# Delta-rule mixer: the finish of a head is cut in two, and its second half is issued behind the next head's q stage

## The chip, the core and the metric

The kernel runs on one core of a Trainium2 chip, as one program that computes one inference step of a small hybrid decoder. Its time is the device time of one execution in microseconds (us). Five engines work side by side, each through its own list of instructions in a fixed order: TensorE (PE in the rows) multiplies and transposes, VectorE (DVE) and ScalarE (ACT) do elementwise work, GpSimd (POOL) does a few elementwise instructions and issues DMA transfers, and SyncE (SP) only issues transfers. Where one engine needs another's result it waits on a semaphore, and everything behind the waiting instruction on that engine waits with it.

## The reference

Two layers, each a mixer and a feed-forward block. The change lies in the mixer of the first layer, the gated delta rule over 8 heads of 128, for a prompt of 1024 tokens and 8 sample sequences of 8 tokens (1088 columns in all):

```python
proj = h @ w_in                                   # q, k, v and a gate, 1024 columns each
qkv = silu(causal_dwconv(qkv, buf, conv_w, conv_b))
q = l2norm(q) * DK ** -0.5;  k = l2norm(k)
# per chunk: decay[i,j] = exp(G_i - G_j) for i >= j
A = strict_lower((k*beta) @ k.T * decay)
sol = triangular_solve(A + I, [v*beta, k*beta*exp(G)])     # uv, w
attn = (q @ k.T) * decay
def step(S, ...):                                 # over the chunks
    u = uv - w @ S
    o = (q*exp(G)) @ S + attn @ u
    S = S * exp(G_last) + kd.T @ u
o = rmsnorm(o, norm_g) * silu(gate)
out = o @ w_out
```

The last two lines are what the change concerns: the output of a head is normalized, gated, and goes to memory until all heads are there, and then the output projection reads it.

## The kernel before

Tokens lie along the columns, 1024 of the prompt and 64 of the samples. Weights and activations of the large products are split into a high and a low part, so each product is three matmuls (L113 to L115 in `dense`); those of the mixer's projections write the tile `pp` and are called plain matmuls here.

Each head is a generator, `gdn_head(h)`, with a `yield` between its stages, and `stage(h, n)` advances head h by n stages. The stages: S1 projects k. S2 loads the decay `dec` (L812), masks it on GpSimd (L814, `affine_select`), takes its exponentials on ScalarE (eight L818, one L819), forms Z from k and k, and transposes k. S3 is the q stage: it projects q, solves 16x16 triangles row by row on VectorE (L881, L883, closed by L884), sends the solution to memory and back in another layout (`td`, issued at L886, and `mg`, issued at L887, which waits for `td`), scales it on ScalarE (L897, L898), multiplies k by q (`pqk`, L905, L908) and applies the decay (L906, L909), transposes q (`pq`, L792) for its sums of squares (L803 on ScalarE) and multiplies q by its decay (L917). S4 projects v and the gate: v goes through a short convolution (L751 and L755 on ScalarE, L758 three times on VectorE), a silu as tanh (L764 on ScalarE) and product (L765 on VectorE), and nine transposes (`pv`, L792). S5 builds the block inverse from Z and `mg`. S6 is the scan over 8 chunks. S7 is the samples' part, with the state update in `sample_state` (`pus`, L716, added at L719), the spill of the samples' state (L1068), and `finish`.

`finish` has a reciprocal square root on VectorE in small steps (L85 to L91), scales the output by it (`ot`, L671, L672), transposes it (`pot`, L676, `pots`, L680), multiplies by the gate (L678, L682), splits the product into a high part (`oh`, L684 on ScalarE) and a low one (L685 on VectorE), and sends both to memory (L686, L687, issued by GpSimd). Small cuts of the modulation work (`adap`, L176, L184) are put in by `ada_step`.

The order of the loop: per head h, S3 and S4 of h, S1 of h+1, S5 of h, S2 of h+1, S6 and S7 of h. This is program order only. A scheduler takes the instructions as they become ready, with program order as the priority, and so writes one fixed list per engine: work of the projections of h+1 fills TensorE between the steps of h. Tiles come from pools with few buffers: PSUM has three of the tag `mx`, which `pus`, `pqk`, `pq`, `pot`, `pots` and `pv` share, and three of `mm` for the plain matmuls. `ot` and `oh` share one buffer, `D5`. The second layer's mixer uses the same `finish`.

Of the kernel before, what the change touches and what calls it, by code (L numbers as in the profile page):

```python
# [42 lines left out]
def trunk_kernel(ctx: ExitStack, tc: tile.TileContext, a: dict, o: dict):  # L43
    nc = tc.nc
# [6 lines left out]
    def big(tag, shape=(128, NTOK), dt=F32, name=None, bufs=None):  # L51
        return main.tile(list(shape), dt, tag=tag, name=name or tag, bufs=bufs or {"xp": 2, "wraw": 3, "whl": 3}.get(tag, 1))

    def small(tag, shape, dt=F32, bufs=1, name=None):
        return sm.tile(list(shape), dt, tag=tag, name=name or tag, bufs=bufs)

    def ps(tag, name=None):
        return psp.tile([128, 512], F32, tag=tag, name=name or tag, bufs={"mm": 3, "mx": 3, "rc": 2}[tag])
# [4 lines left out]
    def cload(name, shape, dt=F32):  # L63
        t = const.tile(list(shape), dt, name="c_" + name)
        nc.scalar.dma_start(out=t, in_=a[name])
        return t

    ident = cload("ident", [128, 128])
# [11 lines left out]
    def rsqrt(y, x, n, tag, p=128):  # L80

        t = small("nwt" + tag, [128, n], bufs=2)[:p]
        xh = small("nwx" + tag, [128, n], bufs=2)[:p]
        sh = small("nws" + tag, [128, n], I32, bufs=2)[:p]
        nc.vector.tensor_scalar(sh, x.bitcast(I32), 1, None, op0=ALU.logical_shift_right)  # L85
        nc.vector.tensor_scalar(y.bitcast(I32), sh, -1.0, float(0x5F3759DF), op0=ALU.mult, op1=ALU.add)
        nc.vector.tensor_scalar(xh, x, -0.5, None, op0=ALU.mult)
        for _ in range(3):
            nc.vector.tensor_tensor(t, y, y, op=ALU.mult)
            nc.vector.tensor_tensor(t, t, xh, op=ALU.mult)  # L90
            nc.vector.scalar_tensor_tensor(y, t, 1.5, y, op0=ALU.add, op1=ALU.mult)  # L91
# [113 lines left out]
    def mod(l, i):  # L205
        return mods[l][:, 8 * i:8 * i + 8, :]

    def fold_scale(l, i, kind, ms=slice(0, 8)):

        m = mod(l, i)[:, ms]  # L210
        nc.vector.scalar_tensor_tensor(
            m, m, 1.0, normw[:, kind, l, ms].unsqueeze(2).to_broadcast([128, ms.stop - ms.start, 9]), op0=ALU.add, op1=ALU.mult)
# [226 lines left out]
    for j in range(4):  # L439
# [6 lines left out]
        for g in GORD:  # L446
            t0, n = GRP[g][0], GP[g]
            sc, sh = mod(0, 1), mod(0, 0)
            pt = big("D10", [128, 2, 512], name="pnt")
            for m in range(2 * j, 2 * j + 2):  # L450
                t = pt[:, m % 2, :n]
                h = hgs[g][:, 0, m, :n]
# [208 lines left out]
    def finish(l, h, ot, ot_s, ss, qe, ncol, gt, ohl, otag):  # L661

        var = small("fvar", [128, 9])
        if qe is None:
            nc.vector.tensor_scalar(var, ss, 1.0 / 128, EPS, op0=ALU.mult, op1=ALU.add)
        else:
            nc.vector.scalar_tensor_tensor(var, ss, 1.0 / 128, qe, op0=ALU.mult, op1=ALU.add)
        rs = small("frs", [128, 9])
        rsqrt(rs, var, 9, "f")
        o3 = ot[:, :NT].rearrange("p (t d) -> p t d", d=128)  # L670
        nc.vector.tensor_tensor(o3, o3, rs[:, 0:8].unsqueeze(2).to_broadcast([128, 8, 128]), op=ALU.mult)  # L671
        nc.vector.tensor_scalar(ot_s, ot_s, rs[:64, 8:9], None, op0=ALU.mult)  # L672
        for b in range(2):
            pt = ps("mx", name="pot")
            for j in range(4):
                nc.tensor.transpose(pt[:, 128 * j:128 * j + 128], o3[:, 4 * b + j, :], ident)  # L676
            gg = gt[:, 512 * b:512 * b + 512]
            nc.vector.scalar_tensor_tensor(gg, pt, ncol, gg, op0=ALU.mult, op1=ALU.mult)  # L678
        pt = ps("mx", name="pots")
        nc.tensor.transpose(pt[:, :NS], ot_s, ident[:64, :64])  # L680
        gg = gt[:, NT:]
        nc.vector.scalar_tensor_tensor(gg, pt[:, :NS], ncol, gg, op0=ALU.mult, op1=ALU.mult)  # L682
        oh = big(otag, dt=F32R, name="oh")
        nc.scalar.activation(oh, gt, AF.Copy)  # L684
        nc.vector.tensor_tensor(gt, gt, oh.bitcast(F32), op=ALU.subtract)  # L685
        nc.gpsimd.dma_start(out=ohl[h][:, 0, :], in_=oh.bitcast(F32))  # L686
        nc.gpsimd.dma_start(out=ohl[h][:, 1, :], in_=gt)  # L687

    smask = cload("smask", [64, 8])
    smask4 = cload("smask4", [64, 4])  # L690
# [35 lines left out]
    gnorm = cload("gnorm", [128, 1])  # L726
# [41 lines left out]
    rest = [(0, i, k) for i in (2, 3, 4) for k in range(8)]  # L768
# [7 lines left out]
    def gdn_head(h):  # L776
# [62 lines left out]
        def evac_k(b, p):  # L839
# [3 lines left out]
            else:  # L843
# [22 lines left out]
            out=Zp, in_=zd[par].rearrange("t x -> (t x)").rearrange("(b y) -> b y", y=2064)[:, :2048].rearrange(  # L866
                "b (j i) -> b j i", i=128)[:, :, 0:16])
# [11 lines left out]
        for i in range(1, 16):  # L879
# [8 lines left out]
                            in_=td[par].rearrange("(t k) (r x) -> (k r) t x", k=8, x=32))  # L888
# [22 lines left out]
        qe = small("gqe", [128, 9], bufs=2)  # L911
# [24 lines left out]
        gt = A(3, "g")  # L936
# [129 lines left out]
        nc.vector.tensor_copy(ot_s, pos[:64, :128])  # L1066
        sample_state(S0, kd_s, u_s, eGLs[:, :, h], v)
        nc.gpsimd.dma_start(out=o["s_gdn"][:, h].rearrange("s k v -> k s v"), in_=S0)  # L1068
        finish(0, h, ot, ot_s, so, qe, gnorm[:, 0:1], gt, ohl0, "D5")

    heads = [gdn_head(h) for h in range(H)]

    def stage(h, n=1):
        for _ in range(n):
            if h < H:
                next(heads[h], None)
# [75 lines left out]
    for b in range(3):  # L1152
        pr = ps("mx", name="pgr")
        ts = [4 * b + j for j in range(4)] if b < 2 else [8]
        for j, t in enumerate(ts):
# [15 lines left out]
                        in_=zero[64:, :].unsqueeze(1).to_broadcast([64, 2, 64]))  # L1171
    X128 = big("D6", [128, 8, 128], name="X128")
    nc.gpsimd.memset(X128, 0.0)
    ohl0 = [drp.tile([128, 2, NTOK], F32, name=f"ohl0{h}") for h in range(H)]

    for h in range(H):
        stage(h, 2 if h else 3)
        stage(h + 1)
        stage(h)
        stage(h + 1)  # L1180
        stage(h, 2)
    fold_scale(0, 2, 1)
    fold_scale(0, 4, 2)
    hgs = out_proj(0, ohl0, 0, 2, 3, 4, "h1")
# [18 lines left out]
    hnorm = cload("hnorm", [128, 1])  # L1203
# [10 lines left out]
    ohl1 = [drp.tile([128, 2, NTOK], F32, name=f"ohl1{h}") for h in range(H)]  # L1214

    def hgrn_head(h):
        par = h % 2
        A = lambda i, name: big(f"A{2 * i + par}", name=name)
        if h:
            q, k, v, gt = A(0, "q"), A(1, "k"), A(2, "v"), A(3, "g")  # L1220
        else:
            q, k, gt = big("cv0", name="q"), big("cv1", name="k"), big("D9", name="g")
# [142 lines left out]
        for b in range(2):  # L1365
# [4 lines left out]
            for j in range(4):  # L1370
# [3 lines left out]
                else:  # L1374
                    nc.vector.scalar_tensor_tensor(Sa[:, t, :], Sa[:, t - 1, :], tot[:, t:t + 1], pu[:, 128 * j:128 * j + 128],
                                                   op0=ALU.mult, op1=ALU.add)
        nc.gpsimd.dma_start(out=o["p_hgrn"][h], in_=Sa[:, 7, :])
        ot = big("D4", [128, NT], name="ot")
        ot_s = small("ot_s", [64, 128])
        so = small("gso", [128, 9])  # L1380
# [22 lines left out]
        nc.vector.tensor_copy(ot_s, pos[:64, :128])  # L1403
        sample_state(S0, kt_s, vt_s, t8, v)
        nc.gpsimd.dma_start(out=o["s_hgrn"][:, h].rearrange("s k v -> k s v"), in_=S0)
        finish(1, h, ot, ot_s, so, None, hnorm[:, 0:1], gt, ohl1, "D4")

    for h in range(H):
        hgrn_head(h)
# [132 lines left out]
```

## Time and profile before

| | us |
|---|---|
| median of three runs | 3267.77 (3267.25 to 3277.91) |
| profiled execution | 3262.61 |
| its span | 3260.8 |
| TensorE busy in the span | 3151.2 (97%) |
| VectorE busy | 1659.1 (51%) |
| ScalarE busy | 1102.4 (34%) |
| GpSimd busy | 276.4 (8%) |

The rows of the section further below come from the profiled execution. Times in them count from the start of its span, and the delta-rule mixer lies at about 90 to 790 us. An idle stretch is written behind an instruction in brackets, with what ended it. The chain of work that ended last is 88% TensorE. One name is misleading: where GpSimd's L887 is said to be released by TensorE, the `td` transfer is what it needs by the code.

### The profile page before, as it was taken

To read this page: it belongs to the slowest core of one execution; us is meant where nothing else is said; L and a number is where in the kernel's file an instruction comes from. 1 tells how busy PE (TensorE), PEld (TensorE's weight loads), DVE (VectorE), ACT (ScalarE), POOL (GpSimd) and SP (SyncE) were. 2 spreads that over 40 slices of the span, in tenths; PEclk is the share of its full clock that TensorE was granted. 3 is DMA by queue.
4 is the path that set the end of the run, shared out by engine and by line. 5 is a ranking of instruction groups with operands and counts; after the bars stand their busy time and mean duration, and the time that the engine had idled before them with its cause. 6 is when DMAs were issued, how large, how long until landed. Compare 5 with 4: busy or idle time off the path is not lost.

```text
span 3260.8 us, 61807 instructions
## 1 busy us (share of the span) xinstructions
PE 3151.2 (97%) x25457; PEld 2933.6 (90%) x25457; DVE 1659.1 (51%) x3783; ACT 1102.4 (34%) x2640; POOL 276.4 (8%) x623
## 2 busy tenths in 40 slices
PE   7999999999899999999998999999999999999998
PEld 5888888888799999999996999999878999999997
DVE  6776777774742333333347555554475233334345
ACT  5444444443433312122234333333333332222222
POOL 0111111110100000000000000000010000000002
PEclk9999999999999999999998999999999999999999
DMA  6333333234322222222223111122521111111113
GB/s 206 99 106 100 102 103 98 79 118 158 97 76 83 84 82 88 82 88 81 92 61 106 64 61 58 59 78 74 199 91 50 46 47 43 46 46 46 41 61 108
DMA packets 164642, 277.94 MB, mean 85 GB/s; under 512 B 20064, under 2 KB 91488, under 8 KB 164360
## 3 DMA queue, kind: packets, MB, share of 16 engines
q1 hardware_dynamic: 145976, 236.28, 22.4%
q0 software_dynamic: 14976, 37.08, 3.8%
q8 instruction: 200, 3.28, 0.4%
q10 hardware_dynamic: 3408, 0.63, 0.1%
q14 instruction: 82, 0.67, 0.1%
HBM read 222.44 MB, written 51.43 MB: 84 GB/s over the span
## 4 chain that ended last, share of the span: by engine, by line
PE 88%; DVE 5%; ACT 2%; DMA 2%; issue 2%; POOL 1%; ACTq 0%; SPq 0%; DVEq 0%; POOLq 0%
PE pp L114 7%; PE pp L113 7%; PE pp L115 7%; PE pu L113 5%; PE pg L113 5%; PE pg L114 5%; PE pg L115 5%; PE pu L115 5%; PE pu L114 5%; PE pd L113 5%; PE pd L115 5%; PE pd L114 5%; PE pf L113 1%; PE pf L114 1%; PE pf L115 1%
## 5 line engine op out<-in xcount | busy, mean ns | idle before, releaser
L114 PE MATMUL pp<-h,wi 128*128 128x384 f32 (+1 forms) x1536 | 515.4, 336 | 1.0 <-DVE h L321 0.9
L113 PE MATMUL pp<-h,wi 128*128 128x384 f32 (+1 forms) x1536 | 515.0, 337 | 0.8 <-DVE q L1236 0.6
L115 PE MATMUL pp<-h,wi 128*128 128x384 f32 (+1 forms) x1536 | 513.1, 335 | 0.8 <-issue 0.8
L113 PE MATMUL pg<-h,wg 128*128 128x384 f32 (+1 forms) x1056 | 346.6, 329 | 0.0
L114 PE MATMUL pg<-h,wg 128*128 128x384 f32 (+1 forms) x1056 | 345.6, 328 | 0.8 <-DVE h L321 0.8
L113 PE MATMUL pu<-h,wu 128*128 128x384 f32 (+1 forms) x1056 | 346.3, 328 | 0.0
L115 PE MATMUL pg<-h,wg 128*128 128x384 f32 (+1 forms) x1056 | 346.0, 328 | 0.0
L115 PE MATMUL pu<-h,wu 128*128 128x384 f32 (+1 forms) x1056 | 344.8, 327 | 0.0
L114 PE MATMUL pu<-h,wu 128*128 128x384 f32 (+1 forms) x1056 | 344.3, 326 | 0.0
L113 PEld LDWEIGHTS pp<-h,wi 128*128 128x128 f32 x1536 | 290.1, 189 | 16.1 <-issue 10.0
L113 PE MATMUL pd<-mh,wd 128*128 128x384 f32 (+1 forms) x912 | 299.5, 330 | 0.0
L115 PE MATMUL pd<-mh,wd 128*128 128x384 f32 (+1 forms) x912 | 297.4, 326 | 0.0
L114 PE MATMUL pd<-ml,wd 128*128 128x384 f32 (+1 forms) x912 | 297.1, 326 | 0.0
L114 PEld LDWEIGHTS pp<-h,wi 128*128 128x128 f32 x1536 | 290.6, 189 | 6.2 <-DVE h L321 1.4
L115 PEld LDWEIGHTS pp<-h,wi 128*128 128x128 f32 x1536 | 290.3, 189 | 4.9 <-issue 2.9
L113 PEld LDWEIGHTS pu<-h,wu 128*128 128x128 f32 x1056 | 198.2, 188 | 7.8 <-issue 6.2
L113 PEld LDWEIGHTS pg<-h,wg 128*128 128x128 f32 x1056 | 199.0, 189 | 6.2 <-issue 4.9
L114 PEld LDWEIGHTS pg<-h,wg 128*128 128x128 f32 x1056 | 199.0, 189 | 2.5 <-issue 1.2
L624 DVE TENSOR_TENSOR facc<-facc,pd 128x384 f32<-128x384 f32 (+1 forms) x192 | 97.6, 510 | 203.1 <-PE pd L115 203.1
L115 PEld LDWEIGHTS pg<-h,wg 128*128 128x128 f32 x1056 | 199.1, 189 | 0.0
L115 PEld LDWEIGHTS pu<-h,wu 128*128 128x128 f32 x1056 | 198.2, 188 | 0.0
L114 PEld LDWEIGHTS pu<-h,wu 128*128 128x128 f32 x1056 | 198.2, 188 | 0.0
(463 smaller groups left out, 5693.9 us busy)
## 6 DMA issues: line engine op xcount, KB each, us to landing
adaw<-in_ada_w SPq DMA_DIRECT2D x96, 512.0 KB, 3.8
wgr<-in_w_gu SPq DMA_DIRECT2D x88, 256.0 KB, 2.8
wur<-in_w_gu SPq DMA_DIRECT2D x88, 256.0 KB, 2.6
wir<-in_w_gin SPq DMA_DIRECT2D x64, 256.0 KB, 2.7
wdr<-in_w_dn SPq DMA_DIRECT2D x64, 256.0 KB, 2.6
wir<-in_w_hin SPq DMA_DIRECT2D x64, 256.0 KB, 2.7
og<-ohl SPq DMA_DIRECT2D x32, 384.0 KB, 6.6
xg<-xd SPq DMA_DIRECT2D x24, 384.0 KB, 5.3
```

The source lines that it names most:

```text
L113: mm(out, wh, rh(k), start=(first and i == 0), stop=False)
L114: mm(out, wh, rl(k), start=False, stop=False)
L115: mm(out, wl, rh(k), start=False, stop=(last and i == len(ks) - 1))
L624: nc.vector.tensor_tensor(am, am, p[:, :n], op=ALU.add)
```

## The change

`finish` does the part up to the scaling and returns the other part as a function, `rest`: transposes, gate, split and spill. In the delta-rule mixer a head gets an eighth stage, S8, that calls it, and the loop runs S8 of head h-1 between S3 and S4 of head h; S8 of the last head follows the loop. The second layer calls `rest` at once, so its program order stays.

```diff
         o3 = ot[:, :NT].rearrange("p (t d) -> p t d", d=128)
         nc.vector.tensor_tensor(o3, o3, rs[:, 0:8].unsqueeze(2).to_broadcast([128, 8, 128]), op=ALU.mult)
         nc.vector.tensor_scalar(ot_s, ot_s, rs[:64, 8:9], None, op0=ALU.mult)
-        for b in range(2):
-            pt = ps("mx", name="pot")
...
-        nc.gpsimd.dma_start(out=ohl[h][:, 0, :], in_=oh.bitcast(F32))
-        nc.gpsimd.dma_start(out=ohl[h][:, 1, :], in_=gt)
+
+        def rest():
+            for b in range(2):
+                pt = ps("mx", name="pot")
...
+            nc.gpsimd.dma_start(out=ohl[h][:, 0, :], in_=oh.bitcast(F32))
+            nc.gpsimd.dma_start(out=ohl[h][:, 1, :], in_=gt)
+        return rest
...
-        finish(0, h, ot, ot_s, so, qe, gnorm[:, 0:1], gt, ohl0, "D5")
+        rest = finish(0, h, ot, ot_s, so, qe, gnorm[:, 0:1], gt, ohl0, "D5")
+
+        yield
+        rest()
...
     for h in range(H):
-        stage(h, 2 if h else 3)
+        stage(h, 1 if h else 3)
+        if h:
+            stage(h - 1)
+            stage(h)
         stage(h + 1)
         stage(h)
         stage(h + 1)
         stage(h, 2)
+    stage(H - 1)
...
-        finish(1, h, ot, ot_s, so, None, hnorm[:, 0:1], gt, ohl1, "D4")
+        finish(1, h, ot, ot_s, so, None, hnorm[:, 0:1], gt, ohl1, "D4")()
```

Since the scheduler decides, the program order alone doesn't tell where the instructions land. The written order of the engines shows it; line numbers of the changed kernel are larger by 2 at L676 to L687 and by 3 behind them. Three places, all in the q stage of head 2, where the output of head 1 is finished.

VectorE before, from the state update L719 to the product of q with its decay, L917; `ot` is the output of head 1, `dec` from `pqk` the decayed product of k and q, `v` from `gxp` the convolution, `g` the gate:

```order
L719 TENSOR_TENSOR S_2516<-S_2516,pus 128x512 x2
...
L884 COPY fs<-fs 72x16x16
...
L671 TENSOR_TENSOR ot<-ot,frs 128x1024
...
L758 SCALAR_TENSOR_TENSOR v<-gxp,c_gcw,v 128x1024
L678 SCALAR_TENSOR_TENSOR g<-pot,c_gnorm,g 128x512 x2
...
L758 SCALAR_TENSOR_TENSOR v<-gxp,c_gcw,v 128x1024
L906 TENSOR_TENSOR dec<-pqk,dec 128x512
L685 TENSOR_TENSOR g<-g,oh 128x1088
L906 TENSOR_TENSOR dec<-pqk,dec 128x512
L909 TENSOR_TENSOR dec<-pqk,dec 64x64
L758 SCALAR_TENSOR_TENSOR v<-gxp,c_gcw,v 128x1024
L917 TENSOR_TENSOR q<-q,eg 128x1088
```

VectorE now (L722 is L719, L909 is L906, L912 is L909, L920 is L917, L887 is L884, L680 is L678, L761 is L758, L687 is L685):

```order
L722 TENSOR_TENSOR S_2516<-S_2516,pus 128x512 x2
...
L909 TENSOR_TENSOR dec<-pqk,dec 128x512
...
L909 TENSOR_TENSOR dec<-pqk,dec 128x512
...
L912 TENSOR_TENSOR dec<-pqk,dec 64x64
...
L920 TENSOR_TENSOR q<-q,eg 128x1088
...
L887 COPY fs<-fs 72x16x16
L671 TENSOR_TENSOR ot<-ot,frs 128x1024
...
L680 SCALAR_TENSOR_TENSOR g<-pot,c_gnorm,g 128x512 x2
...
L761 SCALAR_TENSOR_TENSOR v<-gxp,c_gcw,v 128x1024
...
L687 TENSOR_TENSOR g<-g,oh 128x1088
L761 SCALAR_TENSOR_TENSOR v<-gxp,c_gcw,v 128x1024
...
L761 SCALAR_TENSOR_TENSOR v<-gxp,c_gcw,v 128x1024
```

L906, L909 and L917 have moved ahead of L671 and of L884, and the three L758 all come behind L671 as before, the first of them now behind L678.

ScalarE before, from the split of the output (`oh`) to the exponentials of the next head's decay:

```order
L684 ACTIVATE oh<-g 128x1088
L897 ACTIVATE mg<-mg,c_m16e 128x16x16
L898 ACTIVATE mg<-mg,c_m16e 64x16
L897 ACTIVATE mg<-mg,c_m16e 128x16x16
L898 ACTIVATE mg<-mg,c_m16e 64x16
L803 ACTIVATE junk,gqe<-pq 128x128 x6
L764 ACTIVATE gxp<-v 128x1088
...
L106 ACTIVATE wi<-wir 128x512
L940 ACTIVATE tg<-pp 128x384
L818 ACTIVATE dec<-dec,nG 128x128 x6
```

ScalarE now, behind the last convolution input (L686 is L684, L821 is L818, L900 and L901 are L897 and L898, L767 is L764):

```order
L106 ACTIVATE wi<-wir 128x512
L686 ACTIVATE oh<-g 128x1088
L821 ACTIVATE dec<-dec,nG 128x128 x3
L900 ACTIVATE mg<-mg,c_m16e 128x16x16
L901 ACTIVATE mg<-mg,c_m16e 64x16
L900 ACTIVATE mg<-mg,c_m16e 128x16x16
L901 ACTIVATE mg<-mg,c_m16e 64x16
L821 ACTIVATE dec<-dec,nG 128x128 x4
L106 ACTIVATE wi<-wir 128x512
L821 ACTIVATE dec<-dec,nG 128x128
L767 ACTIVATE gxp<-v 128x1088
```

All eight exponentials of the next head's decay, which followed the tanh of v, now come ahead of it, three before and five behind the scaling of `mg`. This is so in heads 2 to 6. In head 1 two of them come ahead of the tanh; there, and in heads 6 and 7, the split `oh` comes behind the scaling of `mg`.

GpSimd before, from the spill of the samples' state to the mask of the next head's decay:

```order
L1068 DMA out_s_gdn<-S_2516 128x8x128
L747 COPY gxs<-gbuf 128x8x3
L745 DMA gbuf<-in_gbuf 128x24
L886 DMA td<-fs 72x512
L887 DMA mg<-td 128x9x32
L972 MEMSET fs 32x8x32
L686 DMA ohl_913<-oh 128x1088
L687 DMA ohl_913<-g 128x1088
L814 AFFINE_SELECT dec<-dec 128x1024
```

GpSimd now (L889 and L890 are L886 and L887, L817 is L814):

```order
L1071 DMA out_s_gdn<-S_2516 128x8x128
L889 DMA td<-fs 72x512
L890 DMA mg<-td 128x9x32
L975 MEMSET fs 32x8x32
L817 AFFINE_SELECT dec<-dec 128x1024
L688 DMA ohl_913<-oh 128x1088
L689 DMA ohl_913<-g 128x1088
L750 COPY gxs<-gbuf 128x8x3
L748 DMA gbuf<-in_gbuf 128x24
```

The mask L814 stood behind the two spills of the output and now stands ahead of them, directly behind the two transfers of the triangles' solution and a memset.

On TensorE, `pqk` stands directly behind `pus` now, `pq` follows with a few plain matmuls between, then come `adap` and `pot`; of plain matmuls, 71 stood between `pus` and `pv` in head 2, and 80 do now.

## Rows read from the trace of the kernel before

**Rows 1.** Waits of TensorE, 100 to 830 us: what waits for what: total us, times, longest.

```profile
PE pv L792 <- DVE v L765: 6.6, 5, 1.6
PE pot L676 <- DVE ot L671: 3.6, 8, 0.6
PE pq L792 <- DVE dec L906: 3.1, 2, 2.1
```

**Rows 2.** Windows: us, busy PE, PEld, DVE, ACT, POOL (instructions), TensorE clock, DMA share, GB/s.

```profile
200.00:790.00 590.00, 570.12 (x5741) 503.32 (x5742) 413.00 (x1026) 254.18 (x818) 91.01 (x196) 0.99 0.34 109
221.30:224.70 3.40, 3.40 (x23) 3.40 (x24) 3.16 (x6) 1.67 (x7) 1.13 (x2) 1.00 0.06 14
725.80:729.20 3.40, 3.40 (x14) 3.31 (x15) 2.12 (x4) 1.84 (x10) 1.08 (x2) 0.51 1.03 353
1713.70:1717.10 3.40, 3.40 (x25) 2.45 (x29) 1.97 (x4) 2.07 (x10) 0.27 (x1) 1.00 0.98 296
```

**Rows 3.** Timeline of TensorE: start, length, line, tiles, count, [idle before <- releaser].

```profile
221.29 1.20 PE L792 MATMUL pv<-c_ident,v 128*128 128x128 f32 x9 [1.57 <-DVE v L765]
...
285.59 1.16 PE L716 MATMUL pus<-v 32*128 32x128 f32 x16
...
293.04 1.09 PE L676 MATMUL pot<-c_ident,ot 128*128 128x128 f32 x8 [0.54 <-DVE ot L671]
...
304.21 0.33 PE L115 MATMUL pp<-h,wi 128*128 128x384 f32 x1
304.38 0.34 PE L113 MATMUL pp<-h,wi 128*128 128x384 f32 x1
305.88 1.20 PE L792 MATMUL pv<-c_ident,v 128*128 128x128 f32 x9 [1.16 <-DVE v L765]
...
725.72 1.03 PE L792 MATMUL pq<-c_ident,q 128*128 128x128 f32 x4 [2.07 <-DVE dec L906]
...
1713.64 0.44 PE L113 MATMUL pf<-mh,wd 128*128 128x384 f32 x1 [2.48 <-DVE facc L370]
```

**Rows 4.** Timeline of VectorE in the q stage of head 2.

```profile
287.39 1.27 DVE L719 TENSOR_TENSOR S<-S,pus 128x512 f32<-128x512 f32 x2
...
291.05 0.40 DVE L884 COPY fs<-fs 72x256 f32<-72x256 f32 x1
...
299.53 1.26 DVE L758 SCALAR_TENSOR_TENSOR v<-gxp,c_gcw,v 128x1024 f32<-128x1024 f32 x1
...
304.53 1.29 DVE L765 SCALAR_TENSOR_TENSOR v<-gxp,v 128x1088 f32<-128x1088 f32 x1 [1.68 <-ACT gxp L764]
```

**Rows 5.** Timeline of ScalarE in the q stages of heads 1, 2, 6 and 7.

```profile
215.35 0.51 ACT L897 ACTIVATE mg<-mg,c_m16e 128x256 f32<-128x256 f32 x1 [3.73 <-DMA mg<-td]
...
295.92 1.11 ACT L684 ACTIVATE oh<-g 128x1088 fp32r<-128x1088 f32 x1 [4.03 <-DVE g L682]
299.93 0.52 ACT L897 ACTIVATE mg<-mg,c_m16e 128x256 f32<-128x256 f32 x1 [2.90 <-DMA mg<-td]
...
303.39 1.11 ACT L764 ACTIVATE gxp<-v 128x1088 f32<-128x1088 f32 x1
...
308.90 1.85 ACT L818 ACTIVATE dec<-dec,nG 128x128 f32<-128x128 f32 x6
...
639.68 0.51 ACT L897 ACTIVATE mg<-mg,c_m16e 128x256 f32<-128x256 f32 x1 [2.86 <-DMA mg<-td]
...
722.80 0.51 ACT L897 ACTIVATE mg<-mg,c_m16e 128x256 f32<-128x256 f32 x1 [4.25 <-DMA mg<-td]
```

**Rows 6.** GpSimd's timeline, heads 1 and 2; then L814's eight durations, ns min/median/max.

```profile
211.72 1.03 POOL L887 DMA_DIRECT2D mg<-td  x1 [5.88 <-PE pqk L905]
...
291.87 0.55 POOL L886 DMA_DIRECT2D td<-fs  x1
296.88 1.04 POOL L887 DMA_DIRECT2D mg<-td  x1 [4.46 <-PE pqk L905]
...
L814 POOL TENSOR_SCALAR_AFFINE_SELECT dec<-dec x8: 1087/1100/1679, 109.1 to 651.6; 128x1024 f32<-128x1024 f32 x8
```

More of the change, by code (lines that the diff above doesn't have):

```diff
@@ L672, in finish @@
         nc.vector.tensor_scalar(ot_s, ot_s, rs[:64, 8:9], None, op0=ALU.mult)
-        for b in range(2):
-            pt = ps("mx", name="pot")
[L675 to L685, printed above, removed]
-        nc.gpsimd.dma_start(out=ohl[h][:, 0, :], in_=oh.bitcast(F32))
-        nc.gpsimd.dma_start(out=ohl[h][:, 1, :], in_=gt)
+        def rest():
+            for b in range(2):
+                pt = ps("mx", name="pot")
+                for j in range(4):
+                    nc.tensor.transpose(pt[:, 128 * j:128 * j + 128], o3[:, 4 * b + j, :], ident)
+                gg = gt[:, 512 * b:512 * b + 512]
+                nc.vector.scalar_tensor_tensor(gg, pt, ncol, gg, op0=ALU.mult, op1=ALU.mult)
+            pt = ps("mx", name="pots")
+            nc.tensor.transpose(pt[:, :NS], ot_s, ident[:64, :64])
+            gg = gt[:, NT:]
+            nc.vector.scalar_tensor_tensor(gg, pt[:, :NS], ncol, gg, op0=ALU.mult, op1=ALU.mult)
+            oh = big(otag, dt=F32R, name="oh")
+            nc.scalar.activation(oh, gt, AF.Copy)
+            nc.vector.tensor_tensor(gt, gt, oh.bitcast(F32), op=ALU.subtract)
+            nc.gpsimd.dma_start(out=ohl[h][:, 0, :], in_=oh.bitcast(F32))
+            nc.gpsimd.dma_start(out=ohl[h][:, 1, :], in_=gt)
+        return rest
     smask = cload("smask", [64, 8])
```

## The prediction

> **What bounds the kernel now.** I read the profile in four steps. First the waits of TensorE over the whole delta-rule mixer, because TensorE is the engine that is nearly always busy: three kinds of wait touch the change. The transposes `pv` of v wait for VectorE's L765 (6.6 us in 5 waits), the transposes `pot` of a head's output for L671 (3.6 us in 8), and the transposes `pq` of q for L906, which frees their PSUM buffers (3.1 us in 2) [rows 1]. Second the windows: between 200 and 790 us TensorE is busy 570.12 of 590.00 us, so 19.9 us are idle in the stretch that holds seven of the eight heads [rows 2]. That is the most that any order of the same work could win there, and slightly more than 0.5% of the time. Third the engine rows around one q stage, that of head 2, for the chain that ends in `pv` [rows 3 to 6]. Last the granted clock behind each wait: after the 2.07 us wait at 725.72 it was 0.51 for 3.4 us, after the 1.57 us wait at 221.29 it stayed 1.00, and after a 2.48 us wait much later it also stayed 1.00 [rows 2, 3]. A fall costs about half of 3.4 us, 1.7 us. So a wait of two us or more may cost almost double, and one of 1.5 us or less only itself.
>
> **What the change moves.** No instruction is added or removed. Seven of eight heads' outputs (all but the last) are now transposed and gated after the next head's `pqk`, `pq` and `q*eg`. The scheduler's written order says where this lands.
>
> *The pot waits go.* In head 2 `pot` used to start at 293.04, right behind L671 [rows 3]. VectorE now has two L906, L909 and L917 ahead of L671 and three L759 fewer, which I estimate at 1.9 us, so L671 would be done at 294.9. TensorE has `pqk` and both `pq` ahead of `pot` now, but seven plain matmuls fewer; I work its arrival to 295.05. So seven of the eight waits go, 7/8 of 3.6: -3.1 us. The bound is no gain, if L671 slips by 0.7 us more.
>
> *The pq waits go.* L906 now stands directly behind L719 in VectorE's order, ahead of L671, L678, L685: the two waits of 3.1 us in heads 6 and 7 leave, and with them the fall of the clock behind the longer one [rows 2, 3]: -3.1 and -1.7 us.
>
> *pqk gets a wait.* It stands directly behind L716, with no plain matmul between them, and needs PSUM buffers that L719 frees. In head 2 L716 starts at 285.59 and lasts 1.16, so the first half of `pqk` would run to about 287.65, and the first half of L719 (1.27 for both, from 287.39) is done about 288.05 [rows 3, 4]. I take 0.4 us, in seven heads: +2.8 us. Bounds: 0 and 0.8. An interruption of the plain matmuls less saves about 0.1 a head, an estimate: -0.7.
>
> *pv waits longer, the term that decides.* Before, ScalarE's tanh L764 of v ran at 303.39, and the eight exponentials L818 of the next head's decay stood behind it, at 308.90 [rows 5]. Now all eight of L818 (in heads 2 to 6; two in head 1, none in head 7) and the four L897/L898 stand ahead of L764. L818 needs GpSimd's L814, which stands behind L887, and L887 waits for the `td` transfer; L897 waits for the `mg` transfer that L887 starts. Work head 2 through. VectorE's L884 ends near 293.65, 2.2 us later than its 291.05 plus 0.40 [rows 4], because L906, L909 and L917 come ahead; `td` starts at 293.7. It took 5.0 us from the issue at 291.87 to L887 at 296.88, and 6.4 in head 1 (5.88 idle behind an issue of 0.56) [rows 6]. With 4.6 (nearest the 5.0, a little less because the issue comes longer after the spill of S ahead of it), L887 is at 298.3, L814 (1.10) ends about 300.8, `mg` lands about 301.35, 3.05 after L887 as before (296.88 to 299.93) [rows 5, 6]. ScalarE then does three L818 (1.85 for six), the L897 set of about 1.2 (an estimate from its 0.52), four L818, one L106 of about 0.55, one L818: 305.05, then L764 1.11 and L765 1.29, and `pv` starts at about 307.5 [rows 4, 5]. TensorE used to arrive at 305.88 less 1.16; nine plain matmuls at 0.17 (304.21 to 304.38) are moved ahead of `pv`, the `pqk` wait is added, the `pot` wait gone: 306.05 [rows 3]. The wait is 1.5. With the 6.4 of head 1 it would be 3.3, with the 3.05 that `mg` takes it would be 0.1.
>
> In heads 1, 6 and 7 another link comes into the chain: ScalarE has L684 behind the L897 set, VectorE has L685 and the last L758 behind L684, and L764 needs that L758. From the landing of `mg` on: L897 set 1.2, L684 1.1, L685 and L758 1.2 each (L685 reckoned as L758), L764 1.1, L765 1.2, sum 7.0, with 0.4 for a gate tanh or some L818 in heads 6 and 7. Head 1: 215.35 plus 7.1 is 222.5, TensorE arrives about 220.8, wait 1.7. Head 6: 639.68 plus 8.0 is 647.7, arrival 645.5, wait 2.2. Head 7: 722.80 plus 7.4 is 730.2, arrival 727.2, wait 3.0 [rows 4, 5]. So `pv` waits 1.7 + 4 x 1.5 + 2.2 + 3.0 = 12.9 where it waited 6.6: +6.3. Head 7 thus keeps nothing of its `pq` gain.
>
> *The clock.* Heads 6 and 7 wait over 2 us now, and I count one more fall among heads 1 to 5: 3 x 1.7 = +5.1.
>
> The spill of a head's output comes about 2 us later; its reader, the output projection, comes after all heads, and the last head's spill is where it was, so I cost it at nothing.
>
> Sum: -3.1 -3.1 -1.7 +2.8 -0.7 +6.3 +5.1 = +5.6 us on the profiled execution's 3262.6, 3268.2. The median of the runs shown, 3267.8, is 5.2 above that execution, so the forecast is 3273.
>
> A rule of the Trainium skill speaks against the change. The row first: L814 takes 1.10 in the median and 1.68 at most over eight [rows 6]; before, it ran beside VectorE's work at the end of the stage, and now it falls among L758 and L685, which read two operands in SBUF. "SBUF — State Buffer", section "Who interferes with whom", has it that a VectorE instruction with two SBUF inputs and a GpSimd instruction that reads SBUF share a port, and that one then stands still until the other is through. By it L814, or an L758, would end up to one L758 (1.26) [rows 4] later in heads 2 to 5, some 5 us in sum and 3278. The trace agrees in kind, with the 0.6 by which its longest L814 exceeds its median; the sum above goes without it.
>
> **Rivals.** 0.5%, 16.3 us, is about what a measurement of this kernel can tell from no change.
>
> A. *The transfers come early.* If `td`, issued longer after the spill ahead of it, lands in 3 us in heads 2 to 5, the exponentials are through before VectorE's last L758 and `pv` hardly waits there: 4 x 1.4 less, and no fall in these heads: 5.6 - 5.6 - 1.7 = -1.7, 3266. For it: `mg`, of as many bytes, lands in 3.05 [rows 5, 6]. Against: the two `td` of rows 6 took 5.0 and 6.4.
>
> B. *Slower: tanh of v behind the exponentials.* The same chain, with `td` at 6.4: `pv` waits 3.3 in heads 2 to 5, and the clock falls in all seven heads. +7.2 for the waits and 4 x 1.7 = 6.8 for the falls on top of 5.6: +19.6, 3287. It becomes slower than the bound from a `pv` wait of about 2.5 in heads 2 to 5, a `td` of 5.6. For it: head 1's 6.4. Against: head 2's was 5.0, and a wait of 3.3 is twice what any of the five `pv` waits was [rows 1].
>
> C. *The clock keeps up.* The wait of 2.48 us that kept 1.00 [rows 2, 3] shows that two us need not bring it down. Without falls but that of head 7: 5.6 - 3.4 = +2.2, 3270.
>
> D. *Faster.* The stalls go and nothing follows: this needs 16.3 of the 19.9 idle us, with waits in stages that the change doesn't touch included. 3250.
>
> **How the numbers follow.** Forecast 0.52 (its own range 3267 to 3279), A 0.18, C 0.14, B 0.13, D 0.03. Faster by over 0.5%: D, 0.03. Slower: B, 0.13. The rest, 0.84, within. The range from 3262 to 3286 leaves out D, half of B and the far side of A.
>
> **What would show it.** In the profile after: no wait of `pot`, and none of `pq` for L906; a wait of about 0.4 of `pqk` for L719 in each head; L764 directly behind an L818 in heads 2 to 6, and behind the chain L897, L684, L685, L758 in heads 1 and 7; `pv` waits of 1.5 to 3. The forecast is wrong if `td` lands in under 3.5 us or over 5.6, if `pot` still waits, or if L897 of head 7 comes before 720. If `pv` doesn't wait at all in heads 2 to 5, the ScalarE order wasn't the bound.

## The result, and the profile after

The changed kernel takes 3292.14 us (median, 3290.16 to 3296.16) where the kernel before takes 3267.89: ratio 1.0065 with the interval [1.0049, 1.008]. That is slower by 0.65% (the interval begins at 0.49%), and outside the predicted range, whose upper end was 3286. Its profiled execution took 3293.74 us, with a span of 3292.0.

Waits of TensorE after, 100 to 860 us (what waits for what: total us, times, longest), which answer to [rows 1]:

```profile
PE pv L795 <- DVE v L768: 20.5, 7, 3.8
...
PE pX L968 <- issue: 4.3, 2, 3.3
PE pqk L908 <- DVE S L722: 1.9, 7, 0.4
...
PE pp L115 <- issue: 1.6, 1, 1.6
...
PE pV L983 <- issue: 1.1, 1, 1.1
PE pot L678 <- DVE ot L671: 0.7, 1, 0.7
```

The row of `pq` is gone, `pot` waits only for the last head, `pqk` has the wait that was forecast. But `pv` waits in all seven heads, 20.5 us where it waited 6.6. Three of the seven in the timeline of TensorE, heads 1, 2 and 6:

```profile
223.68 1.17 PE L795 MATMUL pv<-c_ident,v 128*128 128x128 f32 x9 [3.85 <-DVE v L768]
...
314.81 2.15 PE L795 MATMUL pv<-c_ident,v 128*128 128x128 f32 x9 [3.27 <-DVE v L768]
...
669.60 1.17 PE L795 MATMUL pv<-c_ident,v 128*128 128x128 f32 x9 [2.43 <-DVE v L768]
```

The other heads wait 3.30 (head 3), 2.18, 3.31 and 2.20 us. In head 2 the transposes themselves took 2.15 instead of 1.17, at a lower clock. The windows behind these three waits and the whole mixer (us, busy PE, PEld, DVE, ACT, POOL with counts, TensorE clock, DMA share, GB/s), which answer to [rows 2]:

```profile
224.50:228.50 4.00, 4.00 (x22) 3.08 (x20) 2.25 (x6) 0.97 (x4) 0.00 (x0) 0.57 0.00 0
```

```profile
313.50:320.50 7.00, 5.69 (x24) 5.25 (x28) 4.25 (x7) 0.77 (x3) 0.11 (x1) 0.51 0.13 41
```

```profile
669.60:673.00 3.40, 3.40 (x25) 3.40 (x26) 3.18 (x8) 1.36 (x3) 0.12 (x2) 1.00 0.03 11
90.00:830.00 740.00, 700.72 (x6787) 621.24 (x6787) 499.12 (x1243) 311.14 (x1001) 113.29 (x238) 0.97 0.33 105
```

Behind the waits of heads 1 and 2 the granted clock fell to the lower of its two levels (0.51 in the second window, so 1.2 of 2.4 GHz); behind that of head 6 it stayed at 1.00. Adding up half a microsecond times one less the granted clock over half-microsecond windows of 90 to 830 us gives what the low clock cost: 20.5 us after, 6.83 before (1.1 and 0.5 of it fall into waits, where a low clock costs nothing). Call this the clock's loss. And call the mixer's stretch the time from TensorE's first transposes of k to its last `pot`: 667.34 us before, 692.32 after. The stretch is 25.0 us longer; 13.7 of them are the clock's, 11.3 are left. The two profiled executions differ by 31.1 us (3293.74 and 3262.61), so 6.2 more lie outside the stretch, where the program order is unchanged; the four runs of the kernel before alone spread over 10.7 us.

The chain of head 2 on the four other engines, which answers to [rows 4 to 6]. Everything lies 5.43 us later than before (L719 at 287.39 has become L722 at 292.82). VectorE:

```profile
292.82 1.27 DVE L722 TENSOR_TENSOR S<-S,pus 128x512 f32<-128x512 f32 x2
...
298.71 0.39 DVE L887 COPY fs<-fs 72x256 f32<-72x256 f32 x1
...
305.30 1.28 DVE L761 SCALAR_TENSOR_TENSOR v<-gxp,c_gcw,v 128x1024 f32<-128x1024 f32 x1
307.10 2.11 DVE L761 SCALAR_TENSOR_TENSOR v<-gxp,c_gcw,v 128x1024 f32<-128x1024 f32 x1
313.37 1.29 DVE L768 SCALAR_TENSOR_TENSOR v<-gxp,v 128x1088 f32<-128x1088 f32 x1
```

GpSimd:

```profile
299.41 0.56 POOL L889 DMA_DIRECT2D td<-fs  x1 [3.16 <-DVE fs L887]
304.54 1.03 POOL L890 DMA_DIRECT2D mg<-td  x1 [4.58 <-DMA td<-fs]
...
305.84 2.29 POOL L817 TENSOR_SCALAR_AFFINE_SELECT dec<-dec 128x1024 f32<-128x1024 f32 x1
```

SyncE, which only issues:

```profile
299.25 0.38 SPq L947 DMA_DIRECT2D S<-in_s_gdn  x1
299.72 0.53 SPq L815 DMA_DIRECT2D dec<-gd  x1
300.35 0.37 SPq L169 DMA_DIRECT2D adaw<-in_ada_w  x1
```

ScalarE:

```profile
308.17 0.99 ACT L821 ACTIVATE dec<-dec,nG 128x128 f32<-128x128 f32 x3 [4.23 <-POOL dec L817]
309.06 0.50 ACT L900 ACTIVATE mg<-mg,c_m16e 128x256 f32<-128x256 f32 x1
...
310.26 1.27 ACT L821 ACTIVATE dec<-dec,nG 128x128 f32<-128x128 f32 x4
...
311.95 0.39 ACT L821 ACTIVATE dec<-dec,nG 128x128 f32<-128x128 f32 x1
312.24 1.10 ACT L767 ACTIVATE gxp<-v 128x1088 f32<-128x1088 f32 x1
```

Read from the end: `pv` waits for L768, that for the tanh L767, and ScalarE is busy from 308.17 until the tanh with work for other purposes: exponentials of the next head's decay, and the scaling of `mg`. The last input of the tanh, L761 at 307.10, was done at 309.21; the tanh ran 3.0 us later, and `pv` waited 3.27. ScalarE stood idle 4.23 us ahead of that work, for the mask L817, which stands behind L890, and that came 5.13 us after the issue of `td`. One thing more: the loads of S and of the decay are issued within 0.4 us of `td`. Before, the decay's load was issued at 302.55, long after `td` had landed:

```profile
294.81 0.38 SPq L944 DMA_DIRECT2D S<-in_s_gdn  x1
302.55 0.33 SPq L812 DMA_DIRECT2D dec<-gd  x1
```

It needs the buffer that L917 (`q` times `eg`) leaves, and the change put that product (now L920, ended at 298.7) ahead of `td`.

### The profile page after: what moved, and what is told of

The parts are those of the page before. It is cut to its first block, busy times and chain, and to the rows that moved or that the text cites. A ratio compares the mean times of both kernels' runs of the same rounds, so it can differ in the third digit from the quotient of the medians.

```text
span 3292.0 us, 61820 instructions
## 1 busy us (share of the span) xinstructions
PE 3172.1 (96%) x25457; PEld 2951.8 (90%) x25457; DVE 1660.0 (50%) x3783; ACT 1100.3 (33%) x2640; POOL 278.3 (8%) x623
## 4 chain that ended last, share of the span: by engine, by line
PE 87%; DVE 5%; ACT 3%; DMA 2%; issue 2%; POOL 1%; ACTq 0%; POOLq 0%; DVEq 0%
PE pp L114 7%; PE pp L113 7%; PE pp L115 6%; PE pg L113 5%; PE pu L113 5%; PE pg L114 5%; PE pg L115 5%; PE pu L115 5%; PE pu L114 5%; PE pd L113 5%; PE pd L115 5%; PE pd L114 5%; PE pf L113 2%; PE pf L114 1%; PE pf L115 1%
## 5 line engine op out<-in xcount | busy, mean ns | idle before, releaser
L113 PEld LDWEIGHTS pp<-h,wi 128*128 128x128 f32 x1536 | 292.8, 191 | 17.3 <-issue 10.7
```

The lines of the kernel that those rows point to most:

```text
L113: mm(out, wh, rh(k), start=(first and i == 0), stop=False)
```

## Experiments

"T" in the expectations is the reading just given. All ratios are against the kernel before, run on the same chip; e1, e2, e5 and e7 were run on one chip, e8 to e10 and the repeat of e2 on a second, e11, e12 and the repeat of the changed kernel on a third, e13 on a fourth. The changed kernel itself came out at 1.0065 and, repeated, at 1.0098, with intervals that do not meet, so ratios of different groups are not to be compared more finely than about 0.3%.

**Order on ScalarE alone.** e1 issues the next head's exponentials behind the tanh of v; e2 does that and puts the scaling of `mg` behind it too.

```diff
+        tanh[kind, h] = nc.scalar.activation(xp, dst, AF.Tanh, scale=0.5)
...
+        with behind_tanh(h - 1):        # tc.issue_after(tanh[2, h - 1].ins)
             for t in range(8):
                 nc.scalar.activation(d3[:, t, :], d3[:, t, :], AF.Exp, bias=nG[:, t, h:h + 1])
...
+        with behind_tanh(h):            # e2 alone
+            for e in range(2):
+                nc.scalar.activation(XTc[:, :, :, e, :], cp[:, 0:8], AF.Copy, scale=m16e[:, e:e + 1])
```

> The changed kernel with one edit: on ScalarE the nine exponentials of the next head's decay are issued behind the tanh of v. TensorE's order stays word for word. Theory T (the wait of pv grew because the tanh stands behind exponentials that wait for GpSimd's mask, and the mask for the td transfer): in heads 2 to 5 the pv waits of 3.27, 3.30, 2.18 and 3.31 us fall to about 0.4 each (then the landing of mg and the last L758 decide), with them about 8 us of low clock in these heads; heads 1, 6 and 7 keep their waits (3.85, 2.43, 2.20), since there the tanh waits for L758 behind L685 behind L684 behind the scaling of mg. 3292 - 10.5 - 8 = about 3273. Rival P (GpSimd's mask and VectorE's convolution step slow each other, 2.11 where one takes 1.27): that overlap stays, so the waits stay near 2.5 and the time near 3288. Rival L (td is issued 2 us later, since L906 and L917 come ahead of L884): the tanh still follows the scaling of mg, so the waits fall by a third only, 3284.

> As e1, and the four scalings of mg (L897, L898) are issued behind the tanh of v too, so neither L684 nor the tanh has a transfer ahead of it on ScalarE. Theory T: all seven pv waits, 20.5 us in sum, fall below 0.5 each, and of the low clock only head 0's 5 us and the 1.7 us behind the issue stall of the last head's inverse stay; the pot and pq waits stay away. About 3292 - 18 - 12 = 3262, under the kernel before (3268) by the 6 us of its pot and pq waits. Rival P: heads 1 to 5 keep about 0.8 us each from the slowed convolution step, 3268. Rival M (the scaling of mg, put later, becomes late for the block inverse): a new wait of the first pV for mg of 1 to 2 us in each head, 3272 or more.

e1: 3279.39 us, 1.0028 [1.0012, 1.0045]; `pv` waits 11.8 us. e2: 3267.75, 0.9988 [0.9977, 0.9999]; `pv` waits in three heads:

```profile
PE pv L800 <- DVE v L773: 1.2, 3, 0.4
```

So the order of ScalarE carries the loss: with tanh ahead of both groups, 19.3 of the 20.5 us leave and the change as a whole costs nothing. The exponentials alone account for less than half of the waits: in heads 2 to 5 12.1 us became 4.0, in heads 1, 6 and 7 8.5 became 7.8. The scaling of `mg`, which waits for its transfer, holds the tanh up by itself.

**Without the mask** (e5), the decay's exponentials replaced by those of a constant from head 1 on, which wait only for the load.

```diff
-        nc.gpsimd.affine_select(out=d3, in_=d3, ...
+        if h < 1:
+            nc.gpsimd.affine_select(out=d3, in_=d3, ...
...
-            nc.scalar.activation(d3[:, t, :], d3[:, t, :], AF.Exp, bias=nG[:, t, h:h + 1])
+            nc.scalar.activation(d3[:, t, :], d3[:, t, :], AF.Exp, **(dict(bias=low, scale=0.0) if h else ...
```

> The changed kernel without GpSimd's mask of the decay in heads 1 to 7 and with a constant in place of the decay's exponentials' argument (its output is not the reference's); ScalarE still does the same nine instructions at the same place ahead of the tanh. So the exponentials wait for the decay's load alone, and nothing on GpSimd runs beside VectorE's convolution steps. Theory T: the exponentials are through before mg lands, pv waits in heads 2 to 5 fall to 0.5 to 1, about 3275. Rival P: the same fall here, and every L758 back at 1.27 us from 2.1; e1 against this run tells T from P. Rival L: no more than the mask's own 1.1 to 2.3 us per head, waits of 1 to 2, 3282.

3291.72 us, 1.0063 [1.0048, 1.0078]: no gain; `pv` waits 19.3. T's expectation for it was wrong. ScalarE in its head 2:

```profile
305.15 0.99 ACT L825 ACTIVATE dec<-dec,low 128x128 f32<-128x128 f32 x3 [1.51 <-DMA dec<-gd]
...
307.61 0.51 ACT L904 ACTIVATE mg<-mg,c_m16e 128x256 f32<-128x256 f32 x1 [1.46 <-DMA mg<-td]
...
310.81 1.10 ACT L770 ACTIVATE gxp<-v 128x1088 f32<-128x1088 f32 x1
```

Three exponentials run early now, and ScalarE then stands idle for `mg`. Five more follow its scaling, and the tanh comes as before behind both. In the changed kernel the mask and the landing of `mg` come close together: by the trace's DMA records the scaling of `mg`, held up by the mask through the three exponentials ahead of it, began 1.42, 0.92, 0 and 0.21 us after `mg` had landed in heads 2 to 5. Without the mask the landing of `mg` sets the end, and it is nearly as late. What the mask does cost is seen in the groups by line, 195 to 760 us (busy, mean ns of one), after and e5:

```profile
L761 DVE SCALAR_TENSOR_TENSOR v<-gxp,c_gcw,v 128x1024 f32<-128x1024 f32 x21 | 31.4, 1495 | 0.3 <-ACT v L758 0.3
```

```profile
L764 DVE SCALAR_TENSOR_TENSOR v<-gxp,c_gcw,v 128x1024 f32<-128x1024 f32 x21 | 26.8, 1277 | 0.3 <-ACT v L761 0.3
```

With the mask five of the 21 convolution steps take 2.11 to 2.53 us, each at a time when a mask runs; the mask took 1.10 in the median before and 1.11 to 2.29 in heads 2 to 5. Without it all of them are back at 1.28. This is the slowing that the prediction set aside, up to 1.25 us a step. What it adds to the `pv` waits can't be told from their sums (19.3 us without it, 20.5 and 24.1 in two traces of the changed kernel), but it is not what they come from: in e7, below, no mask in heads 1 to 6 takes over 1.11 us and no step over 1.29, and `pv` waits 24.0. The Trainium skill, "SBUF — State Buffer", section "Who interferes with whom", has it that a VectorE instruction with two SBUF inputs contends with a GpSimd instruction that reads SBUF, one of them standing still meanwhile. The trace agrees in kind, with steps 0.83 to 1.25 us longer and a mask up to 1.19; in place of the 5 us that the prediction worked out by that page, the four masks of heads 2 to 5 took 1.9 us more than four of 1.10.

**The finish behind `pv`** (e7): S8 of the last head behind S4 instead of ahead of it.

```diff
-        stage(h, 1 if h else 3)
+        stage(h, 2 if h else 3)
         if h:
             stage(h - 1)
-            stage(h)
```

> The changed kernel with the second half of the finish one stage later in program order: behind S4 (v, pv, gate) instead of between S3 and S4. Transposes, gate, split and spill of the output leave the stretch ahead of pv on all engines; L906 and L917 stay ahead of L671. On ScalarE three exponentials (heads 2 to 5) and the scaling of mg still stand ahead of the tanh, none of L684. Theory T: pv still waits 1 to 2.5 us in heads 2 to 5, since the mask and the landing of mg stay ahead; 0 to 1 in heads 1, 6 and 7, where L684 is out of the chain. About 3278. Rival S (it is the finish's own work between q and pv that makes v late): all waits gone, 3262.

3297.45 us, 1.008 [1.0063, 1.0096]; `pv` waits 24.0 us, up to 4.3. No help, against T's expectation: in heads 2 to 5 the tanh now stands directly behind the scaling of `mg`, and `pv` waits 3.3 to 4.2 us there. The split `oh` and the gate are not what holds the tanh, except in head 7, whose wait fell from 2.20 to 0.77.

**Why `td` is late.** e8 keeps the spill of S behind `mg`; since S is loaded into the spilled buffer, its load comes later too. e11 instead keeps the loads of S and of the decay behind `mg`, on GpSimd, with the spill where it was; e12 does both.

```diff
+        mgd[h] = nc.gpsimd.dma_start(out=mg[:, 0:288]...            # all three
...
+        with tc.issue_after(mgd[h + 1].ins) if h < H - 1 else ...:  # e8, e12, in S8
+            nc.gpsimd.dma_start(out=o["s_gdn"][:, h]..., in_=S0)
...
+        with tc.issue_after(mgd[h - 1].ins) if h else ...:          # e11, e12
+            (nc.gpsimd if h else nc.sync).dma_start(out=dec, in_=gd[0, h:h + 1, :]...)
...
+        with tc.issue_after(mgd[h].ins):                            # e11, e12
+            nc.gpsimd.dma_start(out=S0, in_=a["s_gdn"][:, h]...)
```

> The changed kernel with the spill of the samples' state (512 KB, L1071) moved into the new stage and issued by GpSimd behind mg instead of ahead of td. By the scheduler's order this also puts the tanh of v ahead of the exponentials in heads 2 to 5 again. Theory Q (td took 5.1, 5.7, 4.9 and 6.3 us in heads 2 to 5 instead of the 4.6 reckoned, and mg 6.8 in head 1, because the spill shares the DMA engines with them): td takes 3 to 3.5 us now, mg in head 1 about 3.3, so pv waits under 0.5 in heads 2 to 5, about 1 in head 1, and 1 to 2 in heads 6 and 7, whose L684 still stands behind the scaling of mg: 5 us in sum where the changed kernel waits 20.5, with 6 to 9 us of low clock saved: 3268. Rival L (td and mg have their latency whatever lies ahead of them): td stays at 5 to 6, pv waits in heads 2 to 5 are the 0.7 to 1.3 of e1, head 1 keeps 3.9, 3279.

> The changed kernel with the load of the samples' state (S0) and the load of the next head's decay issued by GpSimd behind mg instead of by SyncE, which issued both within 1 us of td in heads 2 to 5 (S at 299.25, decay at 299.72, td at 299.41 in head 2). What was seen in e8: with the spill away td took 2.8 us in heads 1, 6 and 7 but 4.9 to 5.6 in heads 2 to 5 still. Theory Q2 (those two loads, 512 and 544 KB, decide td in heads 2 to 5): td takes 4 to 4.3 us there, as it does in heads 6 and 7 of the changed kernel, and the decay comes so late that the tanh of v stands ahead of the exponentials: pv waits 0 to 0.5 in heads 2 to 5, the time 3272. Rival A (the modulation's load, adaw, issued at 300.35, or the weights): td stays at 5 to 6, waits of 0.7 to 1.3 as in e1, 3279. In heads 1, 6 and 7 td, 4.2 at most, and pv waits as in e1 (4.0, 1.8, 1.9).

> e11 and e8's moved spill together: no large transfer of GpSimd or of the state and decay is issued around td. Theory Q2: td takes 2.8 us in every head of 1 to 7, so pv waits are under 0.5 in heads 2 to 5; heads 1, 6 and 7 as in e8 (2.7, 1.7, 0.6 or less). 3266. Rival A: td 4 to 5.5 in heads 2 to 5, 3270.

From the issue of `td` to that of `mg`, heads 1 to 7, in us:

| | 1 | 2 | 3 | 4 | 5 | 6 | 7 | `pv` waits | ratio [95%] |
|---|---|---|---|---|---|---|---|---|---|
| before | 6.44 | 5.01 | 5.24 | 5.33 | 4.96 | 4.62 | 4.36 | 6.6 | 1 |
| after | 3.94 | 5.13 | 5.73 | 4.94 | 6.28 | 4.21 | 4.18 | 20.5 | 1.0065 [1.0049, 1.008] |
| e8 | 2.77 | 5.64 | 5.36 | 5.18 | 4.91 | 2.81 | 2.78 | 8.2 | 1.0006 [0.9996, 1.0016] |
| e11 | 3.97 | 2.86 | 2.83 | 2.83 | 2.84 | 4.19 | 4.97 | 3.9 | 0.9974 [0.9963, 0.9985] |
| e12 | 2.82 | 2.88 | 2.83 | 2.82 | 2.81 | 2.81 | 2.79 | 4.7 | 1.0017 [1.0004, 1.003] |

The medians of e8, e11 and e12 are 3271.55, 3264.04 and 3280.38 us. In e8 `td` fell as theory Q expected in heads 1, 6 and 7, to 2.8, and not in heads 2 to 5; e11 came out better than expected, e12 worse.

The spill issued 0.9 to 1.4 us ahead of `td` costs it 1.2 to 1.4 us in heads 1, 6 and 7 (e11's 4.97 has 0.8 us more between the landing and the issue of `mg`, which the profile doesn't explain). In heads 2 to 5 the loads beside it cost it more: without them 2.8, with them 4.9 to 6.3. In e8 the load of S is out of the way (it is issued at 303.87 in head 2, behind `mg`), and `td` still takes 5.64, of which 4.11 to its landing, with the decay's load issued 0.65 us ahead of it; in e11 the modulation weights' load, 512 KB, is still there (291.24, 0.75 us behind `td`) and `td` takes 2.86. So the decay's load, 544 KB, is what slows a `td` of 144 KB, as far as these runs tell: none moves that load alone. In head 1 of the changed kernel it is issued 0.1 us behind `mg` instead, and the scaling of `mg` began 6.75 us after its issue; it was 4.99 in e11 and 3.63 before. GpSimd in head 2 of e11:

```profile
290.49 0.56 POOL L892 DMA_DIRECT2D td<-fs  x1 [4.09 <-DVE fs L890]
293.35 1.03 POOL L893 DMA_DIRECT2D mg<-td  x1 [2.30 <-PE pots L682]
294.38 0.91 POOL L951 DMA_DIRECT2D S<-in_s_gdn  x1
...
297.57 0.55 POOL L818 DMA_DIRECT2D dec<-gd  x1
```

There the exponentials come behind the tanh by themselves (306.37 against 299.60), because the decay isn't there yet, and `pv` of heads 2 to 5 waits for nothing. So its fast `td` and its order on ScalarE come together in this run. e12 frees every `td` and is slower than e11 all the same: it has a wait of the plain matmuls for the gate that neither after nor e11 shows.

```profile
PE pp L113 <- DVE g L947: 8.3, 4, 2.4
```

Its trace shows where this comes from. GpSimd issues the load of S only when the spill of S has landed, and the decay's load behind that, 9.3 us behind `td` in head 2 where it is 7.1 in e11. VectorE's L822 and ScalarE's last exponential L825 wait for the decay, and the gate's last tanh, L946, and product, L947, stand behind them; the plain matmuls wait for that product. It is so in heads 2 to 5 alike; head 2:

```profile
302.01 0.56 POOL L818 DMA_DIRECT2D dec<-gd  x1
...
310.20 0.22 DVE L822 TENSOR_TENSOR dec<-dec,c_dmask 64x64 f32<-64x64 f32 x1 [2.98 <-DMA dec<-gd]
310.45 0.35 ACT L825 ACTIVATE dec<-dec,nG 64x64 f32<-64x64 f32 x1 [5.26 <-DVE dec L822]
310.70 0.47 ACT L946 ACTIVATE tg<-pp 128x384 f32<-128x384 f32 x1
...
312.43 0.44 PE L113 MATMUL pp<-h,wi 128*128 128x384 f32 x1 [2.15 <-DVE g L947]
```

Again an urgent instruction stands behind one that hangs on a load.

**What the divided finish is worth.** e9 is the kernel before with e2's order on ScalarE, so without the division; e10 is e2 with e8's spill; e2 was run again beside them.

> The kernel before with e2's edit alone (exponentials and scalings of mg issued behind the tanh of v), without the divided finish. Theory T: there the tanh of heads 1 to 5 starts behind the scaling of mg and six sums of squares, so pv's 6.6 us of waits fall under 2, the pot and pq waits (3.6 and 3.1 us) stay; the stretch from the first transposes of k to the last pot takes 667.3 - 5 = 662 us, and the time is about 3264. The divided finish with the same edit (e2, 658.0) would then be worth 4 us by itself. Rival N (the sums of squares and L758 hold the tanh, not mg): pv waits as before, 3268.

> e2 and e8 together: tanh of v ahead of exponentials and scalings of mg, and the spill of the samples' state behind mg. Theory T: the pv waits are gone already in e2 (1.2 us in sum), so only the mg wait of later heads could gain: the stretch takes 656 to 658 us against e2's 658.0, the time is that of e2 within 2 us. Rival: with the spill later the load of the next head's states (S0, which needs the buffer) comes late and the samples' part waits for it: a new wait of 1 us or more per head in front of pKQ, 3272.

> e2 once more, for a narrower interval against the kernel before: its ratio was 0.9988 (0.9977 to 0.9999). Theory T: the 9.3 us by which its stretch is shorter (658.0 against 667.3) are lasting, ratio 0.997 to 0.999. Rival: e2 only equals the kernel before, ratio 1.000 with an interval that holds it.

e9: 3263.47 us, 0.998 [0.9969, 0.9991]. e10: 3264.64, 0.9977 [0.9967, 0.9988]. e2 again: 3265.13, 0.9988 [0.9973, 1.0003]. Their stretches less the clock's loss are 654.5, 654.4 and 654.2 us; the first e2 had 654.6. In the repeat of e2 `pv` waited 2.8 us in sum, and the clock's loss was 13.7 where it was 3.4 in the first. e9 keeps the waits that the division was to remove:

```profile
PE pot L676 <- DVE ot L671: 3.7, 8, 0.6
PE pq L797 <- DVE dec L909: 3.4, 2, 2.5
```

With the tanh put right, the divided finish is worth nothing that these runs can tell. I expected about 4 us of it. In place of these 7.1 us e2 has 3.8 of `pqk`, `pv` and `pot` waits, and its "issue" waits, which the profile puts down to nothing, are 8.1 us where e9 has 4.9; in sum TensorE stands idle 18.0 us in the stretch of e2 and 18.1 in that of e9. What the "issue" waits come from stays open.

**The changed kernel again, and the best version.** e13 is e2 and e11 in one.

> The changed kernel unaltered, beside the same runs of the kernel before as e11 and e12: ratio 1.005 to 1.008, pv waits of 20 us in sum, 10 to 20 us of low clock between 90 and 830 us. If the waits are those of the first trace but the low clock is under 8 us, the clock's share was chance.

> e2 and e11 together: exponentials and scalings of mg behind the tanh of v on ScalarE, loads of the samples' state and of the next head's decay issued by GpSimd behind mg. The theory (the waits came from the tanh's place on ScalarE and from td among those loads) leaves pv waits under 1 us in sum where e11 has 3.9, all in heads 1, 6 and 7; pot and pq waits stay away. The stretch from the first transposes of k to the last pot, 661.2 in e11 and 658.0 and 667.9 in e2, takes 656 to 660, ratio to the kernel before 0.996 to 0.998. Rival: the mask, now late and alone on GpSimd behind the loads, delays the next head's Z or the scalings of mg delay the first pV: a new wait of 1 us a head, ratio 0.998 to 1.000.

The changed kernel came out at 3300.65, 1.0098 [1.0081, 1.0115], with 24.1 us of `pv` waits; the ratio and the waits are above what was expected. The clock's loss is 15.4 us, in the expected range, and the stretch 687.24, so 671.9 without that loss where the first trace has 671.8: the 11 us beyond the clock come back, and the clock's share was 13.7 us in one execution and 8.5 in the other. Head 3 shows how they hang on `td`, on GpSimd and then on TensorE:

```profile
383.71 0.56 POOL L889 DMA_DIRECT2D td<-fs  x1 [4.11 <-DVE fs L887]
391.11 1.03 POOL L890 DMA_DIRECT2D mg<-td  x1 [6.84 <-DMA td<-fs]
```

```profile
401.14 2.15 PE L795 MATMUL pv<-c_ident,v 128*128 128x128 f32 x9 [5.32 <-DVE v L768]
```

e13 is faster than both kernels: 3260.42 against 3268.67, 0.997 [0.9956, 0.9983]. `pv` waits nowhere; of the waits that the change touches, these are left:

```profile
PE pqk L914 <- DVE S L722: 1.9, 7, 0.4
...
PE pot L678 <- DVE ot L671: 0.7, 1, 0.7
```

Its stretch is 654.05 us with a clock's loss of 5.1, so 648.9 without; before, 660.5; after, 671.8. e13's ratio was measured beside another run of the kernel before than e9's and e10's, and their intervals overlap, as does e11's, so its rank among these four rests on the stretch of one execution each.

## Why the prediction was wrong

The forecast for the profiled execution was +5.6 us; it grew by 31.1, its stretch by 25.0. By the forecast's steps, in the stretch:

- *The pot waits go* (-3.1): 3.6 fell to 0.7, -2.9. Right.
- *The pq waits go* (-3.1): right, no row is left.
- *pqk gets a wait* (+2.8): +1.9, 0.2 to 0.4 in each head. Right in kind, a third too large.
- *pv waits longer* (+6.3): +13.9. This is the term that failed. The chain was the right one, link by link, and it began when it should (`td` at 299.41 is 293.98 in the time of before; I had 293.7); its sizes were not. Heads 2 to 5 were put at 1.5 us each, 6.0, and waited 12.06. There `td` took 5.52 in the mean where I took 4.6, which is 3.7 us in four heads; the masks took 6.3 in sum where I took four times 1.10, which is 1.9; 0.5 is left for the other links. Head 2, which I had worked through, shows it link by link: `td` began 0.3 late and took 0.5 longer, the mask took 1.2 longer, and `pv` could start at 309.4 in the time of before where I had 307.5, while TensorE arrived at 306.1, as I had it. Head 1 was put at 1.7 and waited 3.85: `mg` took 6.75 us from its issue there, 3.63 before. Heads 6 and 7 were put at 5.2 and waited 4.63.
- *The clock* (+5.1, and -1.7 for the fall behind `pq`): 13.7 more instead of 3.4 more. I had placed falls in heads 6 and 7, where no `pv` wait was followed by one, and one in heads 1 to 5, where each was, that of head 2 by a double one (10.2 us in all); two more followed "issue" waits (3.4). The rest cancels: the falls in head 0 and behind another "issue" wait cost 3.4 more, and before's two in head 7 are gone.
- *Fewer interruptions* (-0.7): the waits above make +9.8 of the 11.3 us. In the 1.5 that remain this term can't be told apart from the "issue" waits, which are 7.0 us where they were 3.8.

Why did I take a shorter `td`? I reasoned that the spill ahead of it would lie further back. It does in heads 2 to 5 (4.1 to 5.0 us ahead of `td` where it was 2.0 to 2.8). But I followed L917's move on VectorE only, and not what it sets free: the decay's buffer, and with it a load of 544 KB that now starts beside `td`. That could have been read in the code, where `eg` of one head and `dec` of the next share `D0` or `D2`. With that load and the load of S moved behind `mg` (e11) `td` took 2.8 us in heads 2 to 5, the 3 us of rival A, and `pv` waited for nothing there; in the changed kernel itself its condition did not hold.

Rival B, tanh behind the exponentials with a long `td`, was what happened: 20.1 us of `pv` waits by its prices, 20.5 measured, and 3287 where 3292 was measured. Part of that is luck: it reckoned with a `td` of 6.4 and with falls of the clock in heads 6 and 7, where none came. It had its point of decision at a `td` of 5.6, and 5.52 was close to it; I gave it 0.13, on head 2's 5.0 and the small waits of before. Rival C fell: only two of the seven waits left the clock alone, those of 2.43 and 2.20 us.

What would show the forecast wrong was named as a `td` above 5.6 or under 3.5; two of the four heads were above, and the mean was not. So that sign was too coarse: of the 19.4 us by which the stretch exceeds the forecast, 7.6 are the `pv` waits', of `td`, the mask and head 1's `mg`, and 10.3 the clock's count.

## What to carry to other kernels

When an instruction is moved earlier, look at the buffers it frees as well as at the engine it runs on: a load that waited for one of them starts at once, and here it started beside the transfer that the critical chain was waiting for. On an engine with a fixed order, work that isn't needed soon should not stand ahead of a critical instruction when it hangs on a transfer; issuing it behind (e2) took 19.3 of 20.5 us of waits away, 17.7 in the repeat. And a wait of TensorE is to be priced with the clock behind it: here the clock added 13.7 us in one execution and 8.5 in another to 11.3 us of everything else.

## What the runs showed of the hardware

- The same 144 KB from `td`'s issue to the next instruction took 2.8 us with nothing beside it and 2.8 to 2.9 with a load of 512 KB issued 0.75 us behind it (e11), 3.8 to 5.0 with the spill of S issued 0.9 to 1.4 us ahead (heads 1, 6 and 7 of the divided finish), and mostly 4.1 to 6.3 with the decay's load beside it, in head 3 of three traces 7.4 to 7.8.
- The clock after a wait did not follow its length alone. In the traces of before, after and the repeat every wait of 3.2 us or more between 100 and 830 us was followed by the low clock. Of those from 2.0 to 2.5 us it fell behind 2.07, 2.08, 2.18 and 2.47 and stayed at 1.00 behind 2.06, 2.20, 2.40 and 2.43. The five `pv` waits of before, 1.2 to 1.6 us, kept 1.00, but behind two "issue" waits of 1.1 and 1.6 us (248.38 and 428.19 in after) it was low.
- A convolution step of 1.28 us took 2.11 to 2.53 beside the mask, and the mask, 1.10 alone, up to 2.29.
